# Dilated attention scores: keys ordered by residue, every score product in 64 by 32 tiles, far keys one block later, two query blocks per visit

## The chip, the cores and the metric

One core of one Trainium2 chip runs the whole layer as one program. The metric is the device time of that program in microseconds (us), the median of several runs. A core has TensorE (matrix products, called PE in the profile; its weight loads are PEld), VectorE (DVE), ScalarE (ACT), GpSimd (POOL), and SyncE (SP), which here only issues DMAs. TensorE reads SBUF and writes PSUM, which has eight banks of 512 float32 for each of 128 partitions.

## The reference

One decoder layer over 1024 tokens of width 1024, in float32: RMS norm, one input projection, 8 heads of dilated sliding-window attention (head width 64) beside 4 heads of a gated linear recurrence, an output projection with residual, RMS norm, a gated MLP with a short causal convolution, residual, final norm. The change is in the attention, which merges three branches, each with its own window and dilation, by their softmax denominators:

```
DILATED_PATTERNS = ((128, 1), (512, 4), (2048, 16))
for window, dilation in DILATED_PATTERNS:
    o, m, l = dilated_branch(q, k, v, window, dilation)   # causal, keys at multiples of dilation back
...
w = exp(ms - max(ms));  out = sum(w * os) / sum(w * ls)
```

A query thus sees every key up to 128 back, every fourth up to 512 back and every sixteenth further back. Merged, that is one softmax in which a key counted by n branches has log n added to its score. Beyond 128 back, only keys of the query's own residue modulo 4 matter.

## The kernel before

**Order of the work.** TensorE's instructions run in exactly the order in which the code emits them; the other engines' order comes from a scheduler. Dense products (projections, L460 to L516) use each weight as a high and a low part, three products for one. A `Ring` loads weight pieces on SP (L66, into `raww`), splits them on ACT (L86, `whi`) and on POOL or DVE (L88, `wlo`), and holds five pieces ready. `Fill` is a queue of dense work: `fill.run(us)` emits about so many microseconds of it on TensorE, which is put between the small pieces of attention.

**Attention.** Heads go in pairs p = 0 to 3; queries in blocks b = 0 to 7 of 128. In `qp` the 128 queries of a block lie ordered by residue modulo 4 (4 groups of 32); in `kp` keys lie in natural order. For each p and b:
- `scores(p, b)`: the near part is the block itself and the one before it (256 keys; 128 for b = 0), one product per head with 64 rows and 128 columns of the array (L610). The far part is, for each residue r, 32 queries against the keys r, r + 4, r + 8, ... of all blocks before b (32 b keys): four products per head in 64 by 32 tiles (L615), which read `kp` with a step of four. Each head has a PSUM bank S of tag "s".
- Softmax: DVE adds the mask and takes the extremum (L622), ACT does the exponential and its sum (L624), DVE the reciprocal (L625), POOL the scaling (L626), into P.
- `turn(p, b)`: TensorE transposes P (L641 near, L649 far) into banks of tag "t"; ACT copies the near part (L642), DVE the far part (L653, and L656 into `tri`).
- `values(p, hf)`, once per four blocks: products with V (L669 near, L674 far, L676 for the triangular part of the far keys, in which later blocks have more keys), in a bank of tag "o".

V is made by `v_evac` (L586), which scales a projection into SBUF and also writes it to DRAM (`vd`, L587); `load_far` (L596) reads it back by residue for the far part. q and k are made by `qk_half`, whose products are evacuated by DVE (L570 for q, by residue; L571 for k, contiguous). Tags "s", "t", "o" and "mm" have two banks each. The second halves of q and k for heads 0 and 1 are accumulated in the two "o" banks.

**The loop.** In step (p, b) the code emits `values` if four blocks are done, `scores` of the next block, half a step of dense fill (us/16), `turn` of this block, and another half step. So the scores of a block come one step before its turn. The mask is built at the start: POOL scales and selects (L540 to L543), and DMAs through DRAM (L545 to L549) order its rows by residue.

## Time and profile before

| | |
|---|---|
| Time, median of 3 runs | 1187.13 us (1186.64 to 1187.44) |
| Time of the profiled execution | 1186.35 us |
| Its span in the trace | 1184.6 us |
| TensorE busy | 1174.0 us (99%) |
| DVE, ACT, POOL busy | 866.8, 563.3, 277.1 us |
| TensorE's share of the chain that ended last | 98% |
| Attention (scores, turns, values) | from 40 to 271 us of the span |

A row of the trace's timeline gives the start in us, the duration in us, the engine, the line of the code, the instruction, output<-inputs by the program's names, the array tile as rows*columns with the shape of the moving operand, and how many like instructions were merged (x16). TensorE's durations are modelled and overlap; its start times are the measure. A float32 product is two instructions.

### The profile page before, as it was taken

What the parts mean: (1) busy time and instruction counts of PE and PEld (TensorE: products, weight loads), DVE (VectorE), ACT (ScalarE), POOL (GpSimd) and SP (SyncE); (2) the same over time, 40 slices, a digit from 0 to 9 for tenths busy, and PEclk for the clock granted to TensorE, in tenths of its full rate; (3) what the DMA queues carried; (4) which work ended last, traced back from release to release, by engine and by line L of the source; (5) the groups of instructions that cost most, each with busy time, mean ns of one, the idle gap of its engine ahead of it and who ended that gap; (6) DMA issues with size and microseconds to landing.
All of it is one profiled execution on the core that took longest, in us unless ns stands there. A gap on an engine that the chain in (4) does not pass through costs nothing.

```text
span 1184.6 us, 17883 instructions
## 1 busy us (share of the span) xinstructions
PE 1174.0 (99%) x6422; PEld 964.1 (81%) x6422; DVE 866.8 (73%) x1585; ACT 563.3 (48%) x1103; POOL 277.1 (23%) x244
## 2 busy tenths in 40 slices
PE   9999999999999999999999999999999999999996
PEld 7978787778888888888888888888888888888886
DVE  7543434235887774567998988989888878858987
ACT  8424343566666655446434334343343444444553
POOL 1125253761101035231233122232222200000000
PEclk9999999999999999999999999999999999999999
DMA  7223040332112113440213332233323277435522
GB/s 259 82 76 117 28 125 28 110 121 85 37 37 81 54 63 125 142 141 29 72 54 125 116 111 85 98 125 116 107 73 113 92 241 253 140 96 168 167 94 95
DMA packets 78985, 126.73 MB, mean 107 GB/s; under 512 B 7920, under 2 KB 25104, under 8 KB 78896
## 3 DMA queue, kind: packets, MB, share of 16 engines
q1 hardware_dynamic: 65376, 103.63, 28.0%
q10 hardware_dynamic: 13520, 21.96, 4.9%
q8 instruction: 50, 0.82, 0.3%
q14 instruction: 39, 0.32, 0.1%
HBM read 99.71 MB, written 25.85 MB: 106 GB/s over the span
## 4 chain that ended last, share of the span: by engine, by line
PE 98%; DVE 1%; DMA 0%; POOL 0%; ACT 0%; SPq 0%; issue 0%; DVEq 0%; POOLq 0%
PE p L1136 11%; PE p L1137 11%; PE p L1138 11%; PE ds L1437 3%; PE ds L1435 3%; PE ds L1436 3%; PE po L1040 2%; PE po L1042 2%; PE po L1041 2%; PE da L1437 2%; PE da L1435 2%; PE da L1436 2%; PE S L610 2%; PE S L615 1%; PE piv L514 1%; PE piv L516 1%
## 5 line engine op out<-in xcount | busy, mean ns | idle before, releaser
L88 POOL TENSOR_TENSOR wlo<-raww,whi 128x512 fp32r<-128x512 f32 x137 | 204.6, 1503 | 360.7 <-ACT whi L86 249.2
L86 ACT CAST whi<-raww 128x512 fp32r<-128x512 f32 x276 | 167.9, 617 | 208.3 <-DVE raww L120 65.1
L88 DVE TENSOR_TENSOR wlo<-raww,whi 128x512 fp32r<-128x512 f32 x140 | 101.2, 724 | 24.0 <-ACT whi L86 23.9
L86 ACT CAST whi<-r 128x512 fp32r<-128x512 f32 x70 | 43.6, 623 | 85.4 <-PE ds L1436 50.0
L622 DVE CUSTOM_DVE_ANT_0 P<-S,mask 128x128 f32<-128x128 f32 (+7 forms) x64 | 31.2, 522 | 63.9 <-PE S L615 54.3
L624 ACT ACTIVATE P<-P,st 128x128 f32<-128x128 f32 (+7 forms) x64 | 37.2, 583 | 78.3 <-DVE st L622 78.2
L1437 PE MATMUL ds<-fhi,wlo 128*128 128x512 f32 x160 | 62.3, 389 | 0.0
L1436 PE MATMUL ds<-flo,whi 128*128 128x512 f32 x160 | 62.3, 389 | 0.0
L1435 PE MATMUL ds<-fhi,whi 128*128 128x512 f32 x160 | 62.2, 389 | 0.0
L1136 PE MATMUL p<-b1h,whi 128*128 128x512 f32 x160 | 62.2, 389 | 0.0
L1137 PE MATMUL p<-b1l,whi 128*128 128x512 f32 x160 | 62.2, 389 | 0.0
L1138 PE MATMUL p<-b1h,wlo 128*128 128x512 f32 x160 | 62.2, 389 | 0.0
L88 DVE TENSOR_TENSOR wlo<-r,whi 128x512 fp32r<-128x512 f32 x70 | 48.2, 690 | 19.0 <-ACT whi L86 19.0
L626 POOL TENSOR_SCALAR P<-P,st 128x128 f32<-128x128 f32 (+7 forms) x64 | 35.7, 559 | 108.7 <-DVE st L625 103.0
L1158 DVE SCALAR_TENSOR_TENSOR cv<-g,vec,cv 128x511 f32<-128x511 f32 (+2 forms) x92 | 56.2, 616 | 4.7 <-ACT cv L1155 3.7
L1409 POOL TENSOR_TENSOR facc<-facc,sqf 128x256 f32<-128x256 f32 x2 | 1.5, 738 | 223.0 <-ACT sqf L1408 223.0
L1165 ACT ACTIVATE cv<-cv 128x512 f32<-128x512 f32 x44 | 27.8, 633 | 54.3 <-DVE cv L1158 54.3
L88 DVE TENSOR_TENSOR flo<-rawf,fhi 128x512 fp32r<-128x512 f32 x70 | 48.2, 689 | 4.0 <-ACT fhi L86 4.0
L86 ACT CAST fhi<-rawf 128x512 fp32r<-128x512 f32 x70 | 43.1, 616 | 13.3 <-PE p L1138 4.7
L1435 PE MATMUL da<-fhi,whi 128*128 128x512 f32 x120 | 46.7, 389 | 0.0
L1436 PE MATMUL da<-flo,whi 128*128 128x512 f32 x120 | 46.7, 389 | 0.0
L1437 PE MATMUL da<-fhi,wlo 128*128 128x512 f32 x120 | 46.7, 389 | 0.0
(680 smaller groups left out, 3496.5 us busy)
## 6 DMA issues: line engine op xcount, KB each, us to landing
raww<-in_w_up_dram SPq DMA_DIRECT2D x88, 256.0 KB, 2.9
raww<-in_w_tok_dram SPq DMA_DIRECT2D x52, 256.0 KB, 2.9
rawf<-spT SPq DMA_DIRECT2D x40, 256.0 KB, 2.7
r<-in_w_down_dram SPq DMA_DIRECT2D x40, 256.0 KB, 3.3
raww<-in_w_hg_dram SPq DMA_DIRECT2D x32, 256.0 KB, 2.6
raww<-in_w_out_dram SPq DMA_DIRECT2D x32, 256.0 KB, 2.6
spB<-a ACTq DMA_DIRECT2D x30, 256.0 KB, 2.1
spT<-t ACTq DMA_DIRECT2D x30, 256.0 KB, 2.0
```

The costliest lines, as they stand in the source:

```text
L86: self.pin(self.high(hi[:, :w], raw))
L88: self.pin(low.tensor_sub(lo[:, :w], raw, f32(hi[:, :w])))
L622: DVE.tensor_tensor_reduce(Pt[:, :n], S[e][:, :n], m, -(DH ** -0.5), BIG * 3, op0=ALU.add, op1=ALU.min, accum_out=st[:, 0:1])
L624: ACT.activation(Pt[:, :n], Pt[:, :n], AF.Exp, bias=st[:, 0:1], scale=-1.0, accum_out=st[:, 2:3])
L626: POOL.tensor_scalar(Pt[:, :n], Pt[:, :n], st[:, 3:4], 1.0, op0=ALU.mult, op1=ALU.mult)
L1136: PE.matmul(ps, hi[:, s], bhi, start=(start and n == 0), stop=False)
L1137: PE.matmul(ps, hi[:, s], blo, start=False, stop=False)
L1138: PE.matmul(ps, lo[:, s], bhi, start=False, stop=(stop and n == len(rhs) - 1))
L1158: DVE.scalar_tensor_tensor(dst, x, col(V_CW + j * NFF + f), dst, op0=ALU.mult, op1=ALU.add)
L1435: PE.matmul(ps[d], hi[:, s], ahi, start=(k == 0), stop=False)
L1436: PE.matmul(ps[d], hi[:, s], alo, start=False, stop=False)
L1437: PE.matmul(ps[d], lo[:, s], ahi, start=False, stop=(k == NPAIR - 1))
```

## The change

- `kp` is stored by residue in each block of 128, as `qp` is, and V with it: `v_evac` writes the scaled projection to DRAM, and four DMAs on SP read it back into SBUF by residue. The near part of the mask has its columns ordered by residue too.
- Near scores too are made residue by residue: for each of four groups of 32 queries and each head one product of a 64 by 32 tile against the same 128 or 256 keys. Far scores read runs of 32 neighbouring keys in place of every fourth.
- The far part starts one block later: 32 (b - 1) keys in place of 32 b. The two selections that blanked doubled keys in the mask go.
- S of odd blocks uses a bank of tag "t" for the first head and one of tag "o" for the second.
- The loop goes by pairs of blocks: `values` if due, both blocks' scores, us/8 of fill, turn of the first, us/12, turn of the second, us/24. scores(0, 1) moves to just before the loop; `load_far` of the next pair moves behind the last fill of a pair.

```diff
-        FAR, NEAR = 224, 256
+        FAR, NEAR = 192, 256
...
-        POOL.tensor_scalar(sel[:, FAR:], nat1[:, 0:NEAR], DH ** 0.5, 0.0, op0=ALU.mult, op1=ALU.add)
-        POOL.affine_select(out=sel[:, FAR:], in_=sel[:, FAR:], compare_op=ALU.is_ge, fill=NO, base=0,
-                           pattern=[[1, NEAR]], channel_multiplier=-1)
...
+        POOL.tensor_scalar(in_order(sel[:, FAR:]), by_residue(nat1[:, 0:NEAR]), DH ** 0.5, 0.0, op0=ALU.mult, op1=ALU.add)
...
-                q4 = qp[r0 : r0 + 64, t].rearrange("p (b r l) -> p b r l", r=4, l=32)
-                DVE.tensor_mul(q4, by_residue(ps[0:64]), by_residue(R1[0:64, t]))
-                DVE.tensor_mul(kp[r0 : r0 + 64, t], ps[64:128], R1[64:128, t])
+                for dst, y in ((qp, slice(0, 64)), (kp, slice(64, 128))):
+                    DVE.tensor_mul(in_order(dst[r0 : r0 + 64, t]), by_residue(ps[y]), by_residue(R1[y, t]))
...
-                dst = V[:, t, 4 * g : 4 * g + 4]
-                ACT.mul(dst, ps[:, :256].rearrange("p (h e) -> p h e", h=4), R1T[:, t : t + 1])
-                nc.scalar.dma_start(vd[t * P : (t + 1) * P, 256 * g : 256 * g + 256], dst)
+                x = at.tile([P, 256], F32, tag="vx", name=f"vx{g}_{t}", bufs=2)
+                ACT.mul(x, ps[:, :256], R1T[:, t : t + 1])
+                rows = vd[t * P : (t + 1) * P, 256 * g : 256 * g + 256]
+                nc.scalar.dma_start(rows, x)
+                dst = V[:, t, 4 * g : 4 * g + 4].rearrange("p h e -> p (h e)")
+                for r in range(4):
+                    nc.sync.dma_start(dst[32 * r : 32 * r + 32], rows.rearrange("(l r) e -> r l e", r=4)[r])
...
-            far = 32 * b
+            far = 32 * max(b - 1, 0)
...
-            S = [bank("s", f"S{p}_{b}_{e}") for e in range(2)]
+            S = [bank(("to" if b % 2 else "ss")[e], f"S{p}_{b}_{e}") for e in range(2)]
...
-            for e in range(2):
-                PE.matmul(S[e][:, far:n], qp[rows[e], b * P : (b + 1) * P], kp[rows[e], k0 : k0 + near],
-                          start=True, stop=True)
-            for r in range(4 if b else 0):
-                o = slice(32 * r, 32 * r + 32)
-                for e in range(2):
-                    PE.matmul(S[e][o, 0:far], qp[rows[e], b * P + 32 * r : b * P + 32 * r + 32],
-                              kp[rows[e], r : r + 4 * far : 4], start=True, stop=True)
+            k4 = kp.rearrange("p (b r l) -> p r b l", r=4, l=32)
+            for part in range(2 if far else 1):
+                for r in range(4):
+                    o = slice(32 * r, 32 * r + 32)
+                    for e in range(2):
+                        q = qp[rows[e], b * P + 32 * r : b * P + 32 * r + 32]
+                        if part == 0:
+                            PE.matmul(S[e][o, far:n], q, kp[rows[e], k0 : k0 + near], start=True, stop=True)
+                        else:
+                            PE.matmul(S[e][o, 0:far].rearrange("p (b l) -> p b l", l=32), q,
+                                      k4[rows[e], r, 0 : b - 1], start=True, stop=True)
...
-            if not b:
+            if not far:
                 return
...
-            parts = 1 + (b > 4)
+            parts = 1 + (far > P)
...
-                    PE.matmul(O4[rows[e], 1:, q], v[0:96, hf, r, rows[e]], tri[hf][0:96, e, :, q], start=False, stop=(r == 3))
+                    PE.matmul(O4[rows[e], 2:, q], v[0:96, hf, r, rows[e]], tri[hf][0:96, e, :, q], start=False, stop=(r == 3))
...
         for g in pairs[1]:
             next(g, None)
+        scores(0, 1)
...
-            for b in range(8):
-                while ends:
-                    values(*ends.pop())
-                s = 8 * p + b + 1
-                if s < 32:
-                    scores(s // 8, s % 8)
-                fill.run(us / 16)
-                if b == 3:
-                    load_far(p, 1)
-                turn(p, b)
...
+            for j in range(4):
+                if p or j:
+                    while ends:
+                        values(*ends.pop())
+                    for b in range(2):
+                        scores(p, 2 * j + b)
+                fill.run(us / 8)
+                if j == 2:
+                    load_far(p, 1)
+                turn(p, 2 * j)
+                fill.run(us / 12)
+                turn(p, 2 * j + 1)
+                if j == 3:
+                    fill.run()
+                    if p < 3:
+                        load_far(p + 1, 0)
+                else:
+                    fill.run(us / 24)
+                if j % 2:
+                    ends.append((p, j // 2))
```

## The prediction, made before the change was run

> **What bounds the kernel now.** I read the page first (busy shares, clock, the chain that ended last), then the busy time by stage, then TensorE's instructions in order of time around the edited calls.

> ```profile
> span 1184.6 us, 17883 instructions
> PE 1174.0 (99%) x6422; PEld 964.1 (81%) x6422; DVE 866.8 (73%) x1585; ACT 563.3 (48%) x1103; POOL 277.1 (23%) x244
> PEclk9999999999999999999999999999999999999999
> PE 98%; DVE 1%; DMA 0%; POOL 0%; ACT 0%; SPq 0%; issue 0%; DVEq 0%; POOLq 0%
> ```

> ```profile
> core 0: us, PE busy (x) PEld busy (x) DVE busy (x) ACT busy (x) POOL busy (x), PEclk, DMA share, GB/s
> 40.00:271.00 231.00, 230.94 (x1932) 179.29 (x1931) 91.82 (x274) 104.30 (x248) 106.13 (x120) 1.00 0.28 84
> ```

> The chain that ended last is TensorE for 98%, at full granted clock. The edited code runs from 40 to 271 us; there TensorE is never idle (230.94 of 231.00 us), and no other engine is busy more than 46% (POOL, 106.13 of 231). So a microsecond of TensorE's instruction stream saved here is a microsecond of the span, and any new wait of TensorE costs in full. I therefore cost TensorE start to start: a piece costs the start of what follows it less its own start. (The durations overlap, so they overstate.)

> ```profile
> 86.39 0.39 PE L463 MATMUL p__qk___3_1_1005<-uhi,wlo 128*128 128x512 f32 x1
> 86.71 0.70 PE L610 MATMUL S<-kp,qp 64*128 64x256 f32 x4
> 87.34 0.89 PE L615 MATMUL S<-kp,qp 64*32 64x192 f32 x16
> 88.16 0.50 PE L460 MATMUL p__qk___3_1_1005<-uhi,whi 128*128 128x512 f32 x1
> 88.50 0.39 PE L462 MATMUL p__qk___3_1_1005<-ulo,whi 128*128 128x512 f32 x1
> 88.73 0.40 PE L463 MATMUL p__qk___3_1_1005<-uhi,wlo 128*128 128x512 f32 x1
> ...
> 95.10 1.00 PE L615 MATMUL S<-kp,qp 64*32 64x224 f32 x16
> 96.03 0.39 PE L494 MATMUL pV<-whi,uhi 128*128 128x256 f32 x1
> ...
> 102.49 0.49 PE L610 MATMUL S<-kp,qp 64*128 64x128 f32 x4
> 102.91 0.39 PE L494 MATMUL pV<-whi,uhi 128*128 128x256 f32 x1
> ...
> 113.06 0.33 PE L615 MATMUL S<-kp,qp 64*32 64x32 f32 x16
> 113.32 0.50 PE L460 MATMUL p__qk___4_0_1366<-uhi,whi 128*128 128x512 f32 x1
> ```

> What these rows say:
> - Each float32 product is two instructions (two passes): two heads make four instructions of L610.
> - Near keys (L610, full-width 64 by 128 tiles): 0.63 us for 256 keys (86.71 to 87.34), 0.42 for 128 (102.49 to 102.91). So 0.21 us for 128 more, over two passes: **0.82 ns per key and pass**, the two heads side by side.
> - Far keys (L615, eight 64 by 32 tiles side by side): 0.26 us at 32 keys, 0.82 at 192, 0.93 at 224. Slope (0.93 - 0.26)/192/2 = **1.75 ns per key and pass**, base 0.93 - 2 x 224 x 0.00175 = 0.146 us. Far keys cost twice as much each.
> - Entering scores from dense work: 86.39 to 86.71 is 0.32 us where a dense step takes 0.23 (88.50 to 88.73). Leaving: 88.16 to 88.50 is 0.34. So 0.09 + 0.11 = 0.20 us for each visit to the small tiles.

> **Part 1: the scores.** Before, per head pair: block 0 takes 0.42; blocks 1 to 7 take 7 x 0.63 = 4.41 near, and far with 32 to 224 keys (896 in all) 7 x 0.146 + 2 x 896 x 0.00175 = 4.16. That is 8.99; four pairs 36.0, and 32 visits x 0.20 = 6.4: **42.4 us**.

> After, near keys too go through four column tiles, so there are no full-width score products and no change of tile shape inside a visit; far keys start one block later (0, 0, 32, ..., 192 = 672 in place of 896); two blocks share a visit, 17 visits (the first pair of blocks stays split). Keys per pair: 128 + 7 x 256 + 672 = 2592, each two passes. What a key costs in the new form no row shows; the ends are 0.82 and 1.75 ns. Two things differ between the two old rows: the far read takes every fourth float32 (kp[r::4]), and four column tiles each stream keys of their own. The new far read is runs of 32 neighbouring keys, the new near read wholly contiguous. If the stride made keys dear, the new price is 0.82; if the four column streams did, it is 1.75. I take 0.82, because reads in runs of 32 already run at it:

> ```profile
> 83.63 0.38 PE L649 MATMUL Tf<-ident,P 128*128 128x128 f32 x2
> 83.77 0.47 PE L460 MATMUL p__qk___3_0_918<-uhi,whi 128*128 128x512 f32 x1
> ...
> 110.78 0.39 PE L674 MATMUL O<-k,vs 128*64 128x128 f32 x4
> 111.00 0.34 PE L676 MATMUL O<-tri,vs 96*64 96x96 f32 x4
> 111.17 0.39 PE L674 MATMUL O<-k,vs 128*64 128x128 f32 x4
> ```

> L676 reads three runs of 32 with two column streams (the two heads): 0.17 us for 96 columns, two passes, 0.885 ns per column with everything in it; L674 takes 0.22 for 128, 0.86. Two separate column streams therefore cost nothing and a short run costs nothing. Only going from two streams to four is unseen.

> [...]

> At 0.82: 4 x 2 x 2592 x 0.00082 = 17.0; 17 visits x (0.146 + 0.20) = 5.9; the four far pieces of 32 keys stay at the 0.26 us of their row, 0.06 more each, 0.2. **23.1 us, a gain of 19.3.** At 1.75: 36.3 + 5.9 = 42.2, a gain of 0.2. Each 0.1 ns is worth 2.07 us. More instructions (16 for 4 near) cost nothing in themselves: 16 of them fit in the 0.26 us row, 0.146 of which is base.

> **Part 2: fewer far columns.** The triangular values product covers 64 columns for 96 (L676; 32 columns are 0.22 - 0.17 = 0.05 us): 4 residues x 8 calls x 0.05 = 1.6 us. Far transposes vanish for block 1 and halve for block 5: 8 pairs x 0.14 (83.63 to 83.77) = 1.1 us. Both on TensorE, gain **2.7**.

> **Part 3: the banks of the odd blocks.** S of odd blocks moves from tag "s" to "t" (first head) and "o" (second). In the steady loop the earlier holder of each bank is read by ACT or DVE more than 1 us before. At the start it is not: both "o" banks hold the second halves of q and k for heads 0 and 1, and scores(0, 1) comes right after.

> ```profile
> 48.43 0.70 PE L610 MATMUL S<-kp,qp 64*128 64x256 f32 x4
> 48.53 0.69 DVE L324 TENSOR_TENSOR R<-rt,R 128x512 f32<-128x512 f32 x1 [0.72 <-ACT rt L323]
> 49.14 0.16 DVE L324 TENSOR_TENSOR R1T<-rst,R1T 128x4 f32<-128x4 f32 x1
> 49.96 1.07 DVE L570 TENSOR_TENSOR qp<-p__qk___0_1_293,R 64x512 f32<-64x512 f32 x1
> 51.05 0.69 DVE L571 TENSOR_TENSOR kp<-p__qk___0_1_293,R 64x512 f32<-64x512 f32 x1
> ```

> TensorE stands at scores(0, 1) at 48.43. The first "o" bank is free when DVE has R (49.2) and has run both products of head 0: 1.07 for q and, k being read by residue now as well, 1.07 for k. So about 49.3 + 2.14 + 0.1 = 51.5, with the whole dense queue of TensorE behind it: **a loss of 3.1 us**, once. Bounds: 0 (another bank) to 5.3 (head 1 evacuated first as well).

> k by residue elsewhere: 16 x (1.07 - 0.69) = 6.1 us more on DVE, hidden by its 139 idle us in the stage, except where it delays a reduction (part 4).

> **Part 4: two blocks at once, less lead.** From scores to transposes runs a chain over four engines:

> ```profile
> 195.71 0.50 PE L460 MATMUL p__qk___7_1_2247<-uhi,whi 128*128 128x512 f32 x1
> 195.98 0.59 DVE L622 CUSTOM_DVE_ANT_0 P<-S,mask 128x416 f32<-128x416 f32 x1 [0.80 <-PE S L615]
> 196.49 0.59 DVE L622 CUSTOM_DVE_ANT_0 P<-S,mask 128x416 f32<-128x416 f32 x1
> 197.25 0.63 ACT L624 ACTIVATE P<-P,st 128x416 f32<-128x416 f32 x1
> 197.64 1.24 POOL L626 TENSOR_SCALAR P<-P,st 128x416 f32<-128x416 f32 x2 [7.57 <-DVE st L625]
> 198.01 0.17 DVE L625 RECIPROCAL st<-st 128x1 f32<-128x1 f32 x1 [0.46 <-ACT P L624]
> ```

> Scores end at 195.71, the second head's P is ready at 198.88: 3.2 us. Before, three fill pieces of us/16 (1.95 us), a turn and the next scores lie between scores and turn: over 8 us. After, the first block of a pair has the second block's scores (about 0.7) and us/8 (3.9, in the first pair 4.9): 4.6 us against 3.2, plus about 0.5 because the second block's two reductions stand between the first block's and its reciprocals on DVE. 0.9 us is left; a DVE evacuation (now 2.1 us) or a weight split on POOL ahead of the chain uses it up, and then TensorE waits at the transposes. There are 15 such turns that count; I take a third of them late by 0.4 us: **2.0 us lost**, bounds 0 to 8 (all of them late by half an evacuation).

> **Part 5: V through DRAM, the moved far loads, the mask.** V is written out (as before) and read back by residue: 16 x 4 new issues on SP, each set waiting for its write.

> ```profile
> vd<-V ACTq DMA_DIRECT2D x16, 128.0 KB, 1.7
> vs<-vd SPq DMA_DIRECT2D x8, 256.0 KB, 4.4
> mask<-scratch SPq DMA_DIRECT2D x4, 32.0 KB, 2.5
> ```

> ```profile
> SPq L66 <- POOL wlo L88: 298.3, 79, 14.7
> ```

> Write 1.7, SP issue about 0.4 each, read 2.5: V is some 6 us later. Its readers (values) come over 10 us after the last V block they use. What queues behind the waiting loads on SP is weights (L66). That queue itself mostly waits for old raw tiles to be split (298 us in 79 waits), so it runs five tiles ahead of use; 3 to 4 us of delay sit inside that. Cost 0, bounds 0 to 5 if a weight is caught in the V1 stretches. load_far moves by less than a fill piece, over 10 us before its use; two POOL selects at the start vanish off the path: 0.

> **The sum.** 19.3 + 2.7 - 3.1 - 2.0 = 16.9 us of the profiled execution's 1186.35: 1169.4. The median of the runs stands 0.8 above that execution (1187.13), so **1170.2 us**, 1.4% faster. Least differences that can be told: about 0.2%, or 2.4 us.

> **Rivals.**
> 1. *Four column streams set the 1.75, not the stride* (one mechanism, in all scores). For: all far rows have four streams, no row has four contiguous ones. Against: two streams at full rate. Then the scores gain 0.2 and the sum is 0.2 + 2.7 - 3.1 - 2.0 = -2.2: 1189.3, **slower**. It turns from gain to loss at 1.64 ns per key. Chance 0.13, half of it within 0.2%.
> 2. *The softmax chain becomes the bound*: TensorE waits at each first turn. For: lead falls from 8 to 4.6 us. Against: DVE, ACT and POOL are under half busy. At 0.7 us for 15 turns it costs 10.5 in place of 2.0: 1178.7; it eats the whole gain from 1.25 us each. Chance 0.10.
> 3. *Small tiles issue one after another, each at a floor of its own.* The two transposes take 0.14 us, 0.07 each; at that floor a pass of eight takes 0.56 us, the 14 passes of a pair twice over 15.7 us for 4.25, and four pairs 46 us more: 1216, slower. Against: the 32-key row puts 16 instructions into 0.26 - 0.146 = 0.11 us, 7 ns each. Chance 0.02. [...]

> My forecast has 0.72; the rest (0.03) is unforeseen. The likeliest case's own range is 1165 (no start wait, no late turns) to 1176. To leave no more than 2 in 10 out, the range goes up through rival 2: **1163 to 1186**, which leaves out rival 1 above it. Faster by over 0.2%: 0.80 (0.72 and most of rival 2's 0.10); within 0.2%: 0.10 (half of rival 1, the tail of rival 2); slower: 0.10 (the rest).

> **What would show it.** In TensorE's order of time: a visit for blocks 6 and 7 (256 + 160 and 256 + 192 keys) of about 0.146 + 2 x 864 x 0.00082 = 1.56 us if right, 3.17 by rival 1. One idle gap of TensorE of about 3 us near 48 us, released by DVE's k product. Few waits at the near transposes. L676's successor at 0.12 us for 64 columns. The stage shorter by 15 to 19 us, all after it shifted unchanged. Wrong if visits are long, if idle time stands before the transposes, or if weights arrive late.

## The result, and the profile after

The changed kernel took 1178.03 us (median of 4 runs, 1175.27 to 1178.30) beside 1186.89 (1186.30 to 1187.44) for the kernel before: ratio 0.992, interval 0.9903 to 0.9937. It is 8.9 us faster, well outside the 0.2% that can be told. The forecast was 1170.2, 16.9 us faster; the sign was right, the time lies inside the range, and half of the gain is missing. The profiled execution took 1177.86. Times of runs are medians; one run of the version with both mends, of 5273.77 us, stands far from all others and is left out.

The page of the changed kernel: span, busy shares, clock in 40 slices, chain that ended last.

```profile
span 1176.1 us, 18590 instructions
PE 1159.0 (99%) x6726; PEld 966.1 (82%) x6726; DVE 868.0 (74%) x1577; ACT 561.1 (48%) x1103; POOL 274.1 (23%) x243
PEclk9899999999999999999999999999999999999998
PE 91%; POOL 1%; DVE 1%; issue 1%; ACT 1%; DVEq 0%; POOLq 0%
```

TensorE held 98% of the chain before and holds 91% now: it waits, for POOL among others, and one early slice has a lower clock. The rows to read next are TensorE's waits in the stage (total us, how many, the longest):

```profile
PE piv L515 <- POOL wlo L88: 2.5, 4, 0.8
PE S L617 <- DVE kp L568: 2.5, 1, 2.5
PE pV L495 <- POOL wlo L88: 1.9, 3, 1.5
```

One wait at the start, for DVE's k, as forecast; and seven for the low part of a weight (`wlo`, split on POOL), which the prediction had put at nothing. No wait stands at the near transposes. The busy times by window add the third thing; the last figures of a row are granted clock, DMA share and GB/s:

```profile
40.00:50.00 10.00, 8.03 (x60) 6.94 (x59) 3.96 (x12) 4.97 (x14) 0.74 (x2) 0.99 0.32 95
50.00:60.00 10.00, 9.51 (x66) 8.73 (x67) 3.58 (x9) 1.91 (x6) 0.96 (x2) 0.67 0.21 64
150.00:155.00 5.00, 3.57 (x28) 3.16 (x26) 1.61 (x8) 4.25 (x11) 4.79 (x6) 1.00 0.28 82
155.00:160.00 5.00, 4.80 (x27) 4.80 (x28) 0.74 (x2) 1.06 (x2) 2.61 (x3) 0.66 0.60 174
```

The granted clock falls to 0.67 and 0.66, in the windows in which TensorE stood idle or right behind them. In the records it is 0.5 for 6.83 us from 49.8 and for 3.41 us from 155.6; before, the stage had no such stretch (1.00 from 40 to 271). TensorE's timeline shows both places:

```profile
47.42 0.62 PE L617 MATMUL S<-kp,qp 64*32 64x256 f32 x2
50.49 1.10 PE L617 MATMUL S<-kp,qp 64*32 64x256 f32 x14 [2.46 <-DVE kp L568]
...
52.12 0.41 PE L479 MATMUL pV<-whi,ulo 128*128 128x256 f32 x1
52.33 0.41 PE L477 MATMUL pV<-whi,uhi 128*128 128x256 f32 x1
...
153.44 0.28 PE L494 MATMUL pV<-whi,uhi 128*128 128x256 f32 x1
155.20 0.39 PE L495 MATMUL pV<-wlo,uhi 128*128 128x256 f32 x1 [1.48 <-POOL wlo L88]
```

Two idle times, 2.8 us and 1.76 from start to start, and after the first a product of V takes 0.21 us where it took 0.12. What POOL did ahead of the second:

```profile
150.16 1.27 POOL L630 TENSOR_SCALAR P<-P,st 128x416 f32<-128x416 f32 x2 [4.82 <-DVE st L629]
151.40 1.29 POOL L88 TENSOR_TENSOR wlo<-raww,whi 128x512 fp32r<-128x512 f32 x1
152.66 1.26 POOL L630 TENSOR_SCALAR P<-P,st 128x448 f32<-128x448 f32 x2
153.89 3.72 POOL L88 TENSOR_TENSOR wlo<-raww,whi 128x512 fp32r<-128x512 f32 x3
```

Four scalings of P (two blocks, two heads) come within 3.8 us, with one split between them. The next split ends at about 155.2, when TensorE goes on. One block per step brought two scalings at a time.

The scores themselves, the visit for blocks 6 and 7, and the triangular values with the row behind them:

```profile
147.36 0.66 PE L617 MATMUL S<-kp,qp 64*32 64x256 f32 x16
147.82 0.48 PE L619 MATMUL S<-kp,qp 64*32 64x160 f32 x16
148.09 0.64 PE L617 MATMUL S<-kp,qp 64*32 64x256 f32 x16
148.52 0.53 PE L619 MATMUL S<-kp,qp 64*32 64x192 f32 x16
148.98 0.39 PE L494 MATMUL pV<-whi,uhi 128*128 128x256 f32 x1
...
80.79 0.64 PE L684 MATMUL O<-tri,vs 96*64 96x64 f32 x16
81.36 0.66 PE L617 MATMUL S<-kp,qp 64*32 64x256 f32 x16
```

The visit takes 147.36 to 148.98, 1.62 us; 1.56 was forecast for a price of 0.82 ns, 3.17 for 1.75. Rival 1 was out with this row. L684 takes 0.57 us for four groups with the 0.09 of a change of tile shape, 0.12 each, as forecast.

TensorE's time by the tile that it writes, start to start, summed over the execution (waits stand with the piece ahead of them):

| tile | before | after | difference |
|---|---|---|---|
| S (scores) | 36.05 | 25.08 | -10.97 (the start wait and the half clock on the visit behind it add 3.5 to the after) |
| q and k projections | 94.08 | 91.42 | -2.66 (fewer visits end in them) |
| O (values) | 23.14 | 21.55 | -1.60 |
| far transposes | 6.47 | 5.41 | -1.06 |
| V projection | 48.40 | 53.57 | +5.17 (waits, half clock) |
| piv (the next projection) | 47.05 | 49.74 | +2.69 (waits) |

The sum is -8.4 of the 8.5 us between the two profiled executions.

### The profile page after: what moved, and what is told of

Its sections match the earlier page's. It is cut to its first block, busy times and chain, and to the rows that moved or that the text cites. A ratio compares the mean times of both kernels' runs of the same rounds, so it can differ in the third digit from the quotient of the medians.

```text
span 1176.1 us, 18590 instructions
## 1 busy us (share of the span) xinstructions
PE 1159.0 (99%) x6726; PEld 966.1 (82%) x6726; DVE 868.0 (74%) x1577; ACT 561.1 (48%) x1103; POOL 274.1 (23%) x243
## 4 chain that ended last, share of the span: by engine, by line
PE 91%; POOL 1%; DVE 1%; issue 1%; ACT 1%; DVEq 0%; POOLq 0%
PE p L1147 11%; PE p L1148 11%; PE p L1149 11%; PE ds L1448 3%; PE ds L1447 3%; PE ds L1446 3%; PE po L1051 2%; PE po L1053 2%; PE po L1052 2%; PE da L1448 2%; PE da L1446 2%; PE da L1447 2%; PE O L677 1%; PE S L617 1%; PE Tn L647 1%; PE piv L515 1%
## 5 line engine op out<-in xcount | busy, mean ns | idle before, releaser
L88 POOL TENSOR_TENSOR wlo<-raww,whi 128x512 fp32r<-128x512 f32 x137 | 203.5, 1497 | 380.2 <-ACT whi L86 277.3
L88 DVE TENSOR_TENSOR wlo<-raww,whi 128x512 fp32r<-128x512 f32 x140 | 100.7, 720 | 33.4 <-ACT whi L86 32.2
L88 DVE TENSOR_TENSOR wlo<-r,whi 128x512 fp32r<-128x512 f32 x70 | 48.0, 687 | 19.2 <-ACT whi L86 19.0
L88 DVE TENSOR_TENSOR flo<-rawf,fhi 128x512 fp32r<-128x512 f32 x70 | 48.0, 685 | 4.3 <-ACT fhi L86 4.3
L626 DVE CUSTOM_DVE_ANT_0 P<-S,mask 128x128 f32<-128x128 f32 (+7 forms) x64 | 30.4, 493 | 23.5 <-PE S L619 20.4
## 6 DMA issues: line engine op xcount, KB each, us to landing
raww<-in_w_up_dram SPq DMA_DIRECT2D x88, 256.0 KB, 2.9
raww<-in_w_tok_dram SPq DMA_DIRECT2D x52, 256.0 KB, 3.0
rawf<-spT SPq DMA_DIRECT2D x40, 256.0 KB, 2.7
r<-in_w_down_dram SPq DMA_DIRECT2D x40, 256.0 KB, 3.1
raww<-in_w_hg_dram SPq DMA_DIRECT2D x32, 256.0 KB, 2.6
raww<-in_w_out_dram SPq DMA_DIRECT2D x32, 256.0 KB, 2.6
spB<-a ACTq DMA_DIRECT2D x30, 256.0 KB, 2.1
spT<-t ACTq DMA_DIRECT2D x30, 256.0 KB, 2.0
```

The costliest lines, as they stand in the source:

```text
L88: self.pin(low.tensor_sub(lo[:, :w], raw, f32(hi[:, :w])))
L626: DVE.tensor_tensor_reduce(Pt[:, :n], S[e][:, :n], m, -(DH ** -0.5), BIG * 3, op0=ALU.add, op1=ALU.min, accum_out=st[:, 0:1])
```

## The experiments

My theory after the result: the scores gained nearly what was forecast, and three stalls took half of it back: the start wait, the weight waits from POOL's four scalings in a row, and the half clock behind both idle times. Rivals: the weights are late because of V's read-backs on SP; the clock drops for a reason of its own (what is issued, not that nothing is); and, on the gain, four column streams rather than the stride set the old 1.75 ns. All edits are to the changed kernel unless said; ratios are to the kernel before, which took 1186.41, 1186.34 and 1187.17 us in the three groups of runs.

**The start wait taken away.** scores(0, 1) gets the two "s" banks, as before:

```diff
-            S = [bank(("to" if b % 2 else "ss")[e], f"S{p}_{b}_{e}") for e in range(2)]
+            S = [bank(("to" if b % 2 and (p or b > 1) else "ss")[e], f"S{p}_{b}_{e}") for e in range(2)]
```

> The changed kernel, but scores(0, 1) alone takes the two banks of tag s, as all scores did before. My theory: the 2.8 us in which TensorE waits at 47.7 us is the wait for DVE to empty a bank of tag o, and the 6.8 us at half clock right behind it come from that idle time and cost 3.4 us more. Then both vanish: 6.2 us less than the changed kernel, about 1171.8. Rival (the half clock has another cause, such as the weaker use of the array by 64 by 32 tiles): only the 2.8 us go, about 1175, and the granted clock still falls near 50 us.

1172.14 us (1171.31 to 1172.57), ratio 0.9879 (0.9864 to 0.9894): 5.9 us less than the changed kernel, where the wait itself is 2.83. The window 40 to 60, with TensorE busy throughout and the clock whole:

```profile
40.00:60.00 20.00, 20.00 (x179) 18.29 (x177) 9.19 (x21) 10.92 (x28) 4.90 (x7) 1.00 0.35 103
```

The half clock near 50 went with the idle time. The weight waits stayed (1.76 us at 148.44), but here no half clock followed them: the second stretch is not a fixed price of that wait. So this execution has neither half clock (S takes 3.52 us less and V 3.11), and it gives 1.25 us back in a later dense product, `p`, by a wait for a weight's low part at 618 us that the changed kernel's execution doesn't have.

**The scalings off POOL.**

```diff
-                POOL.tensor_scalar(Pt[:, :n], Pt[:, :n], st[:, 3:4], 1.0, op0=ALU.mult, op1=ALU.mult)
+                DVE.tensor_scalar(Pt[:, :n], Pt[:, :n], st[:, 3:4], 1.0, op0=ALU.mult, op1=ALU.mult)
```

> The changed kernel, with the scaling of P moved from POOL to DVE. My theory: TensorE's seven waits for a low weight part (0.3 to 1.6 us each, 5.5 us in all, between 104 and 259 us) come from POOL, which with two blocks at once has four scalings (2.5 us) in a row between the splits of weights. Then they nearly vanish, with the 3.4 us at half clock behind the longest one (1.7 us of cost): 5 to 7 us less, about 1171 to 1173. Rival (SP is late with the weights because the 64 reads of V stand ahead of them): the waits stay, within 1 us of the changed kernel. Second rival (ACT, with four exponentials in a row, is late with the high parts): the waits shrink by half at most, 1175.

1171.82 us (1171.67 to 1172.07), ratio 0.9877 (0.9863 to 0.9892): 6.2 less. Its waits of TensorE:

```profile
PE S L617 <- DVE kp L568: 2.5, 1, 2.5
PE pV L495 <- POOL wlo L88: 1.2, 2, 1.0
```

All four waits of piv are gone and those of V shrink from 1.9 to 1.2 us. Splits on POOL were late because scalings stood ahead of them. The second rival expected half of the waits at least to stay, if ACT were late with the high parts; 1.2 of 4.4 us stayed. Not all of the 6.2 us is the scalings', though: the half clock behind the start wait lasted 3.41 us here and not 6.83, which is worth 1.7. DVE ran 64 instructions more, 28 us of busy time (895.7 for 868.0), and TensorE waits for none of them in the stage.

**V without the read-backs on SP.** ACT writes V straight to SBUF; its rows then stay in token order, which leaves the ordering by residue of V out:

```diff
-                x = at.tile([P, 256], F32, tag="vx", name=f"vx{g}_{t}", bufs=2)
-                ACT.mul(x, ps[:, :256], R1T[:, t : t + 1])
...
-                for r in range(4):
-                    nc.sync.dma_start(dst[32 * r : 32 * r + 32], rows.rearrange("(l r) e -> r l e", r=4)[r])
+                dst = V[:, t, 4 * g : 4 * g + 4]
+                ACT.mul(dst, ps[:, :256].rearrange("p (h e) -> p h e", h=4), R1T[:, t : t + 1])
...
```

> The changed kernel, with V written by ACT straight into SBUF in token order, as before, without the 64 reads back on SP (the near product then pairs V with the wrong keys; the time alone is asked for). My theory (POOL is late): the seven waits for low weight parts stay, the time within 1.5 us of the changed kernel. Rival (SP's queue delays weights): they go, 5 to 7 us less.

1175.15 us (1174.27 to 1175.58), ratio 0.9904 (0.9887 to 0.992), 2.9 less, which is outside what I expected. But every weight wait stands at the same instruction with the same size (1.76, 1.14, 1.19, 1.15 us for the four long ones). The difference lies in the clock: one half-clock stretch of 3.41 us in place of 6.83 and 3.41. Halving 6.8 us less is worth 3.4 at most, so the read-backs on SP explain no weight wait.

**Both mends together**, the first two edits:

> Both single mends at once: scores(0, 1) in the banks of tag s, scaling of P on DVE. If the two losses are separate, they add: 5.9 + 6.2 = 12.1 us less than the changed kernel's 1178.0, less what both counted (the half clock at 155 us was gone in both, 1.7): 1166 to 1167.5. If they are one loss seen twice (only the half clock), 1171 to 1172.

1166.7 us (1165.71 to 1168.19), ratio 0.9833 (0.982 to 0.9846). The losses were separate in the main: 5.9 and 6.2 apart, which both count the half clock near 155 us (1.7), and 11.3 together. Two weight waits in the V stretches are left, 0.56 and 1.31 us, and there is no half clock in the stage.

**Twelve splits more on DVE** (those of three weight tiles of V; DVE runs 1653 instructions for 1641, POOL 167 for 179), on top of both mends, for the last two waits:

```diff
-        ring.on_vector = ["V1_0"] + [(x, h) for x in ("hf", "hq", "hg") for h in range(NG)]
+        ring.on_vector = ["V1_0", "V1_1", "V1_2", "V1_3"] + [(x, h) for x in ("hf", "hq", "hg") for h in range(NG)]
```

> both_mends, and the splits of the weight pieces V1_1, V1_2 and V1_3 on DVE (0.69 us) in place of POOL (1.28). Two waits for a low part were left with the scaling on DVE, 0.4 us at 103 and 0.3 + 1.2 at 152, behind four splits in a row on POOL. If POOL's rate is what is left, they go: 1.5 to 2 us less than both_mends, about 1165. If not, the same as both_mends.

1165.91 us (1164.71 to 1167.92), ratio 0.9827 (0.9813 to 0.984), 20.4 us under the kernel before: the best version here. Against both mends the runs overlap, so its own step of 0.8 us isn't resolved by time; the trace has no wait of TensorE left in the stage, and the chain is TensorE's again:

```profile
span 1163.4 us, 18551 instructions
PE 98%; DVE 1%; DMA 0%; ACT 0%; issue 0%; DVEq 0%; SPq 0%
```

**Is it idle time that halves the clock?** Dummy products into a spare "mm" bank right ahead of scores(0, 1), first 24 of them, then 12:

```diff
+        warm = bank("mm", "warm2")
+        busy(24)        # second kernel: busy(12)
         scores(0, 1)
```

> The changed kernel, with 24 products of ones (about 2.6 us of TensorE) put in front of scores(0, 1), where it waits 2.8 us for DVE anyway. If the half clock comes from the idle time, the wait stays as long but is filled, the clock stays whole near 50 us, and the time falls by 1.7 (one window of 3.4 us at half clock) to 3.4 (two): 1174.6 to 1176.3. If idle time is not the cause, the clock still falls and the time stays at 1178.

1177.69 us (1175.99 to 1178.04), ratio 0.9922 (0.9908 to 0.9935), above the time I expected. I had mis-sized the fill: 24 products are 48 instructions and ran 5.5 us, about twice the wait, and pushed the rest back by 2.6. The clock did what the theory says (window 47 to 53, clock 1.00):

```profile
47.00:53.00 6.00, 6.00 (x67) 5.78 (x66) 5.04 (x6) 1.09 (x3) 0.00 (x0) 1.00 0.44 127
```

> busy_wait with 12 products in place of 24 (24 turned out to be 48 instructions of 0.11 us, 5.5 us, twice the wait). 12 are 2.7 us, no longer than the wait of 2.8. If idle time sets the half clock, the clock stays whole near 50 us and the time is 1.7 to 3.4 us below the changed kernel: 1174.6 to 1176.3. If not, 1178.

1175.17 us (1174.31 to 1176.46), ratio 0.9898 (0.9882 to 0.9915): 2.9 less than the changed kernel although TensorE still gives the same time away at this point. Useless work in place of idleness keeps the clock near 50 us whole, and that alone is worth 2.9 us by the medians, 1.9 between the two profiled executions. In its profiled execution the 1.76-us wait later on (151.49) was followed by a half clock of 3.41 us from 153.95; the same wait in start_banks, v_direct and busy_wait was not.

**One block per visit.** The new tiles and V, but the old loop (one block's scores ahead, us/16 twice, all S in tag "s"):

```diff
-            for j in range(4):
-                if p or j:
...
-                    for b in range(2):
-                        scores(p, 2 * j + b)
-                fill.run(us / 8)
+            for b in range(8):
+                while ends:
+                    values(*ends.pop())
+                s = 8 * p + b + 1
+                if s < 32:
+                    scores(s // 8, s % 8)
+                fill.run(us / 16)
...
```

> The changed kernel's tiles, key order and V, but the loop of before: one block per visit, us/16 of fill twice, scores one step ahead of their turn, all S banks of tag s. Its banks also take the start wait away, so it compares with start_banks (1172.1). My theory: 15 more visits cost 15 x (0.146 + 0.20) = 5.2 us, and the waits for low weight parts, 5.2 us, go, since two scalings in place of four stand in a row on POOL: about 1172. Rival (the waits come from the new V or from the shorter stage, not from the pairing): the waits stay, 1177.

1170.31 us (1169.66 to 1171.08), ratio 0.9863 (0.9849 to 0.9876): 7.7 us less than the changed kernel. TensorE has no wait in the stage (busy 222.00 of the 222.00 us from 40 to 262). What 15 more visits cost shows against the version with twelve splits more on DVE, which has no wait either: S 1.16, the q and k projections 2.18 and piv 1.06 us more, 4.4 in all, where I had expected 5.2. Against start_banks, which also has no start wait but keeps the weight waits, piv and V cost 2.63 and 2.12 less although piv carries its share of the visits; the weight waits themselves are 5.75 us (piv 3.69 and V 2.06 between start_banks and the version without waits). So pairing the blocks saves 4.4 us of visits and costs 5.75 of waits, unless the work on POOL is made less: then it is worth having (1166.7 and 1165.9 against 1170.3).

**The near products at full width again**, on top of both mends: one 64 by 128 product per head, in place of four 64 by 32 ones; the old products in the new order of keys:

```diff
+            for e in range(2):
+                PE.matmul(S[e][:, far:n], qp[rows[e], b * P : (b + 1) * P], kp[rows[e], k0 : k0 + near],
+                          start=True, stop=True)
...
```

> both_mends (1166.8), with the near scores again as one full-width product per head (64 by 128 tiles) in place of four 64 by 32 tiles; far scores, key order and pairs of blocks stay. It tells what the tiles alone are worth. My theory, from the rows of before: near 0.42 + 7 x 0.63 and far 6 x 0.146 + 2 x 672 x 0.00082 make 6.8 us for a head pair, where the tiled form was measured at 5.4 (21.6 for four): 5.7 us more, 1172.5. Rival (dropping the strided read did it all, the small tiles nothing): 1167.

1170.27 us (1170.02 to 1170.71), ratio 0.9859 (0.9844 to 0.9873). A near piece of 256 keys, up to the start of the far one:

```profile
143.96 0.70 PE L612 MATMUL S<-kp,qp 64*128 64x256 f32 x4
144.59 0.50 PE L618 MATMUL S<-kp,qp 64*32 64x160 f32 x16
```

0.63 us, where the same piece in small tiles took 0.46 (147.36 to 147.82 above). S costs 27.27 us for 21.56, 5.7 more, as expected. The change of tile shape inside a visit is the cost; the price per key is the same (0.82 ns at full width before the change, 0.83 in small tiles, from 0.43 us for 256 keys and 0.27 for 160 at 148.09 and 147.82 us above). Two full-width pieces in a row (128 and 256 keys at 108.08 us, up to 108.94) take 0.86 us, where the same two pieces apart took 0.42 and 0.63. The whole kernel loses 3.6 us, less than 5.7: the last weight waits are gone (V costs 1.63 less). That the slower scores give POOL the time for it is my reading; no run isolates it.

**Stride or four streams?** Two kernels made from the kernel before, whose far reads take other keys than the reference's, so that only their times are of use. First, head pair p reads with a step of p + 1:

```diff
-                              kp[rows[e], r : r + 4 * far : 4], start=True, stop=True)
+                              kp[rows[e], 0 : (p + 1) * far : p + 1], start=True, stop=True)
```

> The kernel before, with the far products of head pair p reading keys at a step of p + 1 in place of 4 (1, 2, 3 and 4 for pairs 0 to 3; wrong keys for the first three; four column tiles as ever). The slope of the far products per key and pass tells the stride from the four column streams. [...] Four column streams: 1.75 at every step. Time: at most 5 us less than the kernel before if steps 1 to 3 are all cheap, none less if streams set it.

1183.45 us in one run. The far rows (16 instructions) and what follows them, 32 keys at steps 1 and 4, then 224 keys at steps 1, 2, 3, 4:

```profile
48.96 0.29 PE L615 MATMUL S<-kp,qp 64*32 64x32 f32 x16
49.18 0.39 PE L477 MATMUL pV<-whi,uhi 128*128 128x256 f32 x1
...
219.96 0.33 PE L615 MATMUL S<-kp,qp 64*32 64x32 f32 x16
220.22 0.50 PE L514 MATMUL piv<-whi,uhi 128*128 128x512 f32 x1
...
93.80 0.61 PE L615 MATMUL S<-kp,qp 64*32 64x224 f32 x16
94.34 0.39 PE L494 MATMUL pV<-whi,uhi 128*128 128x256 f32 x1
...
149.90 0.64 PE L615 MATMUL S<-kp,qp 64*32 64x224 f32 x16
150.47 0.39 PE L494 MATMUL pV<-whi,uhi 128*128 128x256 f32 x1
...
204.32 0.81 PE L615 MATMUL S<-kp,qp 64*32 64x224 f32 x16
205.06 0.50 PE L514 MATMUL piv<-whi,uhi 128*128 128x512 f32 x1
...
259.14 1.00 PE L615 MATMUL S<-kp,qp 64*32 64x224 f32 x16
260.07 0.50 PE L514 MATMUL piv<-whi,uhi 128*128 128x512 f32 x1
```

Step 1: (0.54 - 0.22) / 192 / 2 = 0.83 ns per key and pass. With the unrounded starts, steps 2, 3, 4 give 0.92, 1.32, 1.75. Four contiguous streams run at the near price (0.83 for 0.82 ns); the stride made far keys dear. Step 4 runs at about half the rate of step 1 (1.75 against 0.83 ns), and step 2 already costs 11% more than step 1. These rows give the price of each step, not its cause.

I then thought that the four streams share one supply, so that one stepping stream among four would cost little; a stepping stream that is slow by itself would bring 1.75 ns from the first one on. That they share one was a guess of mine. Second, only the residues r < p step by four:

```diff
-                              kp[rows[e], r : r + 4 * far : 4], start=True, stop=True)
+                              kp[rows[e], 0 : far * (4 if r < p else 1) : 4 if r < p else 1], start=True, stop=True)
```

> The kernel before, with the far products of head pair p stepping by 4 in p of the four column tiles and reading neighbouring keys in the others (wrong keys; pairs 0 to 3 have 0, 1, 2, 3 stepping tiles of each head). [...]

1183.53 us in one run. 224 keys with none, one and three of four tiles stepping:

```profile
93.33 0.61 PE L615 MATMUL S<-kp,qp 64*32 64x224 f32 x16
93.86 0.39 PE L494 MATMUL pV<-whi,uhi 128*128 128x256 f32 x1
...
150.31 0.97 PE L615 MATMUL S<-kp,qp 64*32 64x224 f32 x16
151.21 0.39 PE L494 MATMUL pV<-whi,uhi 128*128 128x256 f32 x1
...
260.38 0.99 PE L615 MATMUL S<-kp,qp 64*32 64x224 f32 x16
261.31 0.50 PE L514 MATMUL piv<-whi,uhi 128*128 128x512 f32 x1
```

0.53, 0.90, 0.93 us; slopes 0.83, 1.77 and 1.77 ns (1.77 with two tiles also). The supply theory falls: one stepping tile of four costs as much as three (0.90 and 0.93 us, 0.53 with none), so a stepping stream is slow by itself, and the pass lasts as long as its slowest tile.

## Why the prediction was right in sign and half in size

Between the two profiled executions 8.5 us were gained, 8.4 less than the 16.9 of the sum. By its steps:

- **Part 1, the scores: right mechanism, price right, about 1 us too large.** The version without any wait gained 20.4 us by the medians (21.1 between profiled executions), where parts 1 and 2 alone say 19.3 + 2.7 = 22.0. The mis-sized term is the visits with short far pieces. In the version with both mends, blocks 2 and 3:

```profile
60.34 0.66 PE L617 MATMUL S<-kp,qp 64*32 64x256 f32 x16
60.79 0.25 PE L619 MATMUL S<-kp,qp 64*32 64x32 f32 x13
...
60.99 0.66 PE L617 MATMUL S<-kp,qp 64*32 64x256 f32 x12
...
61.74 0.50 PE L460 MATMUL p__qk___2_0_782<-uhi,whi 128*128 128x512 f32 x1
```

  The visit takes 1.40 us, where the model of Part 1 (0.146 + 2 x 608 x 0.82 ns, and 0.06 for the piece of 32 keys) says 1.20. Blocks 4 and 5 take 1.51 for 1.35; with larger pieces it fits (blocks 6 and 7: 1.62 for 1.56). The records of blocks 2 and 3 interleave (13 and 12 of 16 stand together), so the excess can't be put on one piece. A short piece alone isn't dear: in one_block, where 32 keys end a visit of their own (113.95 us), they take 0.20, which is the base of 0.146 and 0.05 for the keys. What sets the excess where another block follows, no run isolates. By tile, S gained 14.5 us where the model says 16.3, and the dense pieces around the visits 4.2 (3.14 for q and k, 1.02 for piv) where fewer visits were to give 3.0: Part 1 is 18.7 us, for 19.3.
- **Part 2, fewer far columns: right.** 1.60 and 1.06 us for 1.6 and 1.1.
- **Part 3, the start wait: right, its sequel missed.** 2.83 us for 3.1, released by DVE's k as named. Not foreseen: the clock at half behind it, (1 - 0.67) x 10 us less the half of 0.5 us that was idle anyway, 3.1 us. start_banks has neither.
- **Part 4, late turns: not spent.** 2.0 us were reserved; no wait stands at a near transpose, and rival 2 did not come. The chain did press elsewhere: not on TensorE's turn, but on POOL's queue.
- **Part 5, weights: the step that failed.** "Cost 0, bounds 0 to 5 if a weight is caught in the V1 stretches." The cost was 5.4 us, start to start, over normal steps, in seven waits (0.4, 0.3, 1.6, 0.9, 1.0, 0.3, 0.9; the profile's own idle times, which leave out the slower restart, add up to 2.5 + 1.9). That is just past its bound, and for another cause. I looked at SP's queue, and v_direct shows that it does not matter. I did not cost POOL's own order: two blocks together put four scalings of 0.6 us ahead of splits of 1.3 us, and DVE, ACT and POOL "under half busy" over the stage hid that POOL is 4.79 of 5 us busy from 150 to 155. one_block and scale_on_dve show it from both sides. Behind the 1.76-us wait the half clock took another (1 - 0.66) x 5 = 1.7 us in this execution.

Waits 5.4, half clock 3.1 + 1.7, scores 0.6 short, less 2.0 unspent and 0.3 at the start: 8.5, for the 8.4 missing. Of these, the half clock is in part luck: the 1.7 us fell due in this execution and not in others with the same wait.

Rival 1 fell by the rows of the visits and by far_steps, and rival 3 by the same visits: 16 instructions of 256 keys fit in 0.46 us. The 64 instructions of blocks 2 and 3 took 1.40 us, 22 ns each with their keys in it. A smaller price for each instruction is not ruled out, and could be the excess of Part 1.

## What to carry to other kernels

When a kernel is bound by one engine and work is bunched, read each helper engine's queue in order around the bunch: a low busy share over a stage says nothing of four operations in a row ahead of the one that is waited for. Count an idle time of TensorE at more than its length, here up to twice (2.83 us and 3.1 of half clock, 1.76 and 1.7), and take the bank, or any other resource, whose last reader is early for the first use. Where several small tiles run side by side, make all their moving reads contiguous: one strided stream of four set the time of all here (0.90 us for 224 keys, 0.53 with none).
